# A hybrid decoder step on one core: the last token chunks 430, 430 and 172 wide, and the root of the narrow one on all partitions

## The chip, the cores and the metric

The program runs on one core of one Trainium2 chip. The metric is the device time of one execution in microseconds. The core has TensorE (PE: matmuls; PEld: its weight loads), VectorE (DVE), ScalarE (ACT), GpSimd (POOL) and SyncE (SP), which issues the DMAs; each engine works through its own queue in order, and semaphores join them.

## The reference

One layer of a decoder on 1024 prompt tokens and 8 sample tokens (1032 columns, model width 1024). The change touches the last lines alone: the second half-step FFN and the final norm.

```python
def rmsnorm(x, g):
    y = x * lax.rsqrt(jnp.mean(x * x, axis=-1, keepdims=True) + EPS)
    return y * g
...
x = x + 0.5 * swiglu(rmsnorm(x, ffn1_norm_g), ffn1_w_in, ffn1_w_out)
mix = token_mix(rmsnorm(x, mix_norm_g), ...)      # attention and DeltaNet heads
x = x + mix
gate, up = jnp.split(rmsnorm(x, ffn2_norm_g) @ ffn2_w_in, 2, axis=-1)
x = x + 0.5 * (jax.nn.silu(gate) * up) @ ffn2_w_out
y_prompt, y_sample = rmsnorm(x_prompt_rows, final_norm_g), rmsnorm(x_sample_rows, final_norm_g)
```

## The kernel before

All activations stand transposed: a tile has 128 model rows on the partitions and the 1032 tokens along its columns, so x is eight tiles of 128 x 1032, the row blocks k = 0 to 7. Float32 products are made of three reduced-precision matmuls each (`mm3`, lines 321 to 323): weights and activations are split into a high and a low part in the type float32r, and high x high, high x low and low x high are summed in PSUM. Each of the three loads its own 128x128 weights.

The program's last stage is `ffn_out` (line 706), called with `cb3`: the hidden activations, 22 blocks of 128 (`self.hs`), times the out matrix, 8 row blocks, added to x. The hidden blocks come in five groups of 4, 4, 6, 4 and 4. In the first four groups the loop runs over the row blocks m and, for each, over the three chunks of 344 tokens. In the last group it runs over the chunks first: for each chunk eight row blocks, four hidden blocks, three matmuls, 96 matmuls in all. `one` ends with VectorE's `x<-mm,x` (half the product plus x), then `square` adds up the squares: ScalarE squares into a tile `t`, and GpSimd (k = 1, 2, 3, 5, 6) or VectorE (k = 4, 7, `DVE_SQ`) adds it to `acc`.

After the eighth row block of a chunk, `cb3` starts a background job with that chunk's final norm (`norm`, line 382, `rstd`, line 360):

- three plain float32 matmuls `ps<-ones,acc` sum the squares over the partitions, token blocks of 115 as weights and one column of ones as the moving side, so that the sums come to lie on 115 partitions x 3 columns (each shows as two rows in the profile);
- VectorE makes the reciprocal root of these 115x3 numbers in twelve steps (`nv`, then `rsqrt`, line 331: a shift, a multiply-add on the bits, three rounds of three steps), and writes three diagonal matrices `t<-ident,rsqy`;
- three plain float32 matmuls `ps<-t,ones` broadcast the roots to all partitions, 344 columns (the broadcast);
- ScalarE copies the broadcast to SBUF for GpSimd; VectorE scales six row blocks, x times gain times the broadcast in PSUM (`x<-x,c_norm_g,ps`); GpSimd scales two (`POOL_Y`, k = 1 and 4) in two steps each;
- each row block is stored by a DMA `o_y<-x` on SyncE.

TensorE's queue has the order in which the program is written down. The background jobs are woven in while it is written: each matmul moves on a clock of the program's own (`tick`, line 221, a time in proportion to the columns), each step of a job books time on its engine (`book`, line 208), and the job's next piece is written down when that clock says its input is ready. The order of the other engines is set by the scheduler of the language. Tiles `t` of up to 512 columns have four buffers (`T2`), PSUM three for products and five for the rest.

Of the kernel before, what the change touches and what calls it, by code (L numbers as in the profile page):

```python
# [10 lines left out]
F32 = mybir.dt.float32  # L11
# [3 lines left out]
ALU = mybir.AluOpType  # L15
# [4 lines left out]
P = 128  # L20
D = 1024
KT = D // P
# [3 lines left out]
TT = T + NS  # L26
CW = 344
CHUNKS = [(c * CW, CW) for c in range(3)]
DFF = 2816
NF = DFF // P  # L30
NH = 4
EPS = 1e-6
BW = 1060
CONSTS = ("dist", "sink", "ssink", "conv_w", "conv_st", "negmask", "cum", "a_log", "dt_bias", "gdn_g", "sel", "kvsel")
HW = 258
# [9 lines left out]
PAD = 400.0  # L45
# [13 lines left out]
POOL_Y = (1, 4)  # L59
# [55 lines left out]
class Net:  # L115
# [83 lines left out]
        t = self.tmp.tile([P, 512], F32, tag="t2", name=self.name("t2"), bufs=T2)  # L199
        return t[:, :w]  # L200

    def pmm(self):
        return self.mm.tile([P, CW], F32, tag="mm", name=self.name("mm"))

    def pps(self):
        return self.ps.tile([P, 512], F32, tag="ps", name=self.name("ps"))
# [121 lines left out]
        lo = [self.bt(dt=F32R, s="xnlo") for _ in range(KT)]  # L328
        return hi, lo

    def rsqrt(self, x):
        nc = self.nc
        p, n = x.shape
        y = self.t("rsqy", [P, 16], bufs=3)[:p, :n]
        t = self.t("rsqt", [P, 16], bufs=2)[:p, :n]
        nc.vector.tensor_scalar(t.bitcast(I32), x.bitcast(I32), 1, None, ALU.logical_shift_right)
        nc.vector.tensor_scalar(y.bitcast(I32), t.bitcast(I32), -1.0, float(0x5F3759DF), ALU.mult, ALU.add)
        for _ in range(3):
            nc.vector.tensor_tensor(t, y, y, ALU.mult)
            nc.vector.scalar_tensor_tensor(t, t, -0.5, x, ALU.mult, ALU.mult)  # L340
            nc.vector.scalar_tensor_tensor(y, t, 1.5, y, ALU.add, ALU.mult)
        return y
# [17 lines left out]
    def rstd(self, acc, cs, use):  # L360
        nc = self.nc
        yield PAD
        m = 115 if cs[0][1] > HW else 86
        offs = [[c0, c0 + m, c0 + w - m] for c0, w in cs]
        n = 3 * len(cs)
        ps = self.pps()
        v = self.t("nv", [P, 12])
        for i, o in enumerate(sum(offs, [])):
            self.mmul(ps[:m, i:i + 1], acc[:, o:o + m], self.ones[:, 0:1])
        nc.vector.tensor_scalar(v[:m, :n], ps[:m, :n], 1.0 / D, EPS, ALU.mult, ALU.add)  # L370
        r = self.rsqrt(v[:m, :n])
        for j, (c0, w) in enumerate(cs):
            dgt = self.t2(3 * m)
            for i in range(3):
                nc.vector.tensor_scalar(dgt[:m, i * m:(i + 1) * m], self.ident[:m, :m], r[:, 3 * j + i:3 * j + i + 1], None, ALU.mult)
            yield PAD
            bcs = self.pps()
            for i, o in enumerate(offs[j]):
                self.mmul(bcs[:, o - c0:o - c0 + m], self.ones[:m, :], dgt[:m, i * m:(i + 1) * m])
            use(bcs, c0, w)  # L380

    def norm(self, x, gi, c0, w, acc, out):
        nc = self.nc

        def use(bcs, c0, w):
            rs = self.t2(w)
            nc.scalar.copy(rs[:, :w], bcs[:, :w])
            for k in range(KT):
                y = x[k][:, c0:c0 + w]
                g = self.norm_g[:, gi, k:k + 1]  # L390
                if k in POOL_Y:
                    nc.gpsimd.tensor_tensor(y, y, rs[:, :w], ALU.mult)
                    nc.gpsimd.tensor_scalar(y, y, g, 1.0, ALU.mult, ALU.mult)
                else:
                    nc.vector.scalar_tensor_tensor(y, y, g, bcs[:, :w], ALU.mult, ALU.mult)
                out(k, y)

        yield from self.rstd(acc, [(c0, w)], use)

    def scaled_split(self, x, gi, k, hi, lo, s):  # L400
        nc = self.nc
# [301 lines left out]

        self.builders.append(gen())

    def ffn_out(self, last_cb):
        nc = self.nc

        def one(m, c0, w, whi, wlo, o, f0, g):
            ps = self.pmm()  # L710
            s = slice(c0, c0 + w)
            for j in range(g):
                ks = slice(o + j * P, o + (j + 1) * P)
                h = self.need_op(self.hs, f0 + j)
                self.mm3(ps, whi[:, ks], wlo[:, ks], h[0][:, s], h[1][:, s], j == 0, j == g - 1)
            x = self.need_op(self.xr, m)
            nc.vector.scalar_tensor_tensor(x[:, s], ps, 0.5, x[:, s], ALU.mult, ALU.add)
            self.adv()

        for f0, g in KGROUPS:  # L720
            per = PER[g]
            if f0 + g < NF:
                for m0 in range(0, KT, per):
                    whi, wlo = self.take()
                    for m in range(m0, m0 + per):
                        for c0, w in CHUNKS:
                            one(m, c0, w, whi, wlo, (m - m0) * g * P, f0, g)
                    self.drop()
            else:
                wide = [(self.bt([P, per * g * P], F32R, "whi"), self.bt([P, per * g * P], F32R, "wlo")) for _ in range(KT // per - 3)]  # L730
                ws = [self.take() for _ in range(3)]
                for t in wide:
                    ws.append(self.extra(*t))
                acc = self.bt(s="acc")
                for c0, w in CHUNKS:
                    for m in range(KT):
                        whi, wlo = ws[m // per]
                        one(m, c0, w, whi, wlo, (m % per) * g * P, f0, g)
                        last_cb(self.xr, m, c0, w, None)
                        self.square(acc[:, c0:c0 + w], m, self.xr[m][:, c0:c0 + w])  # L740
                        if c0 + w == TT and m % per == per - 1:
                            if m // per < 3:
                                self.drop()
                            else:
                                self.fr(whi, wlo)
                    last_cb(self.xr, KT, c0, w, acc)
            for f in range(f0, f0 + g):
                self.fr(*self.hs[f])
# [63 lines left out]
    def chunked(self, ws, xhi, xlo, evac, jobs):  # L812
        for c, (c0, w) in enumerate(CHUNKS):
            s = slice(c0, c0 + w)
            if jobs and jobs[c][0]:
                self.wait(jobs[c][0])
            self.settle(KEEP)
            ps = [self.pps()[:, :CW] if jobs and c + i > 0 and c + i < 3 else self.pmm() for i in range(2)]
            for p, (whi, wlo) in zip(ps, ws):
                for k in range(KT):  # L820
                    ks = slice(k * P, (k + 1) * P)
                    self.mm3(p, whi[:, ks], wlo[:, ks], xhi[k][:, s], xlo[k][:, s], k == 0, k == KT - 1)
                if c == 2:
                    self.drop()
            self.due.append((jobs and jobs[c][1], partial(evac, c, *ps)))
            self.settle(KEEP if jobs else 0)

    def proj_chunk(self, wt, c, xhi, xlo, evac):
        whi, wlo = wt
        c0, w = CHUNKS[c]  # L830
        ps = self.pmm()
# [13 lines left out]
    def gates(self, xhi, xlo):  # L845
# [15 lines left out]

        for c0, w in CHUNKS:
            ps = self.pmm()
# [542 lines left out]
    def mix_in(self, xhi, xlo, rs, scr, jobs):  # L1406
# [31 lines left out]
        def evac_kv(c, pk, pv):  # L1438
            ek(pk, *CHUNKS[c])
            ev(pv, *CHUNKS[c])  # L1440
# [153 lines left out]
def build(tc, io):  # L1594
    with ExitStack() as ctx:
        ctx.enter_context(tc.manual_schedule(engines=ORDERED))
        n = Net(tc, ctx, io)
        nc = tc.nc
# [65 lines left out]
        n.mix_out(scr, xd, cb2, done2, gens, ms, ds)  # L1664
        n.ffn_head(xg, xg["rs"], done, hd[1], HEAD[1])
        n.ffn_in(xT, hd[1], lambda: n.out_ops(hd[1], lambda m: xe[:, m, :]), HEAD[1])
        n.ffn_out(cb3)
        n.wait(*jobs3)


# [88 lines left out]
```

## Time and profile before

| | |
|---|---|
| runs shown, us | 2110.12, 2114.11, 2117.31; median 2114.11 |
| the profiled execution's own time, us | 2115.43 |
| its span, first to last instruction, us | 2113.2 |
| mean granted TensorE clock over the span | 0.973 |
| PE busy, share of the span | 96% |
| DVE, ACT, POOL busy, share of the span | 58%, 33%, 28% |
| start of the last chunk's last matmul, us from the span's start | 2098.24 |

Times in the rows are microseconds from the start of the span. A matmul's row runs from its start until its last result is out, so rows of one stream overlap; what a stream costs is read from start to start. A row of the timeline with "x6" holds six like instructions in turn, from the first one's start to the last one's end.

### The profile page before, as it was taken

To read this page: it belongs to the slowest core of one execution; us is meant where nothing else is said; L and a number is where in the kernel's file an instruction comes from. 1 tells how busy PE (TensorE), PEld (TensorE's weight loads), DVE (VectorE), ACT (ScalarE), POOL (GpSimd) and SP (SyncE) were. 2 spreads that over 40 slices of the span, in tenths; PEclk is the share of its full clock that TensorE was granted. 3 is DMA by queue.
4 is the path that set the end of the run, shared out by engine and by line. 5 is a ranking of instruction groups with operands and counts; after the bars stand their busy time and mean duration, and the time that the engine had idled before them with its cause. 6 is when DMAs were issued, how large, how long until landed. Compare 5 with 4: busy or idle time off the path is not lost.

```text
span 2113.2 us, 37138 instructions
## 1 busy us (share of the span) xinstructions
PE 2024.6 (96%) x15062; PEld 1963.6 (93%) x15062; DVE 1222.1 (58%) x2624; ACT 699.8 (33%) x1491; POOL 594.9 (28%) x517
## 2 busy tenths in 40 slices
PE   7799999999999999999999979999999999999997
PEld 6799999999999998787888869899999999999997
DVE  7755555555533544676977874685555555464335
ACT  5233333333211333545243332443333333331112
POOL 3354444341000131332211111245444444200003
PEclk7999999999999999999999979999999999999999
DMA  4112222227322221211212151221222222552112
GB/s 152 60 58 91 81 73 84 86 71 281 113 68 60 84 81 35 69 45 32 67 46 50 57 181 35 97 70 61 86 81 83 79 81 76 194 195 84 55 41 81
DMA packets 109771, 180.81 MB, mean 86 GB/s; under 512 B 35168, under 2 KB 63744, under 8 KB 109584
## 3 DMA queue, kind: packets, MB, share of 16 engines
q1 hardware_dynamic: 109568, 178.41, 26.6%
q8 instruction: 118, 1.93, 0.4%
q14 instruction: 53, 0.43, 0.1%
q0 software_dynamic: 32, 0.03, 0.0%
HBM read 135.60 MB, written 43.85 MB: 85 GB/s over the span
## 4 chain that ended last, share of the span: by engine, by line
PE 40%; DVE 8%; DMA 1%; issue 1%; SPq 1%; ACT 0%; POOL 0%; DVEq 0%; ACTq 0%; POOLq 0%
PE mm L321 6%; PE mm L322 6%; PE mm L323 6%; PE ps L528 4%; PE ps L530 4%; PE ps L529 4%; PE ps L243 3%; PE mm L528 2%; PE mm L530 2%; PE mm L529 2%; DVE conv L89 1%; DVE inv L89 1%; SPq L102 1%; DVE Tb L89 1%; DVE x L89 1%
## 5 line engine op out<-in xcount | busy, mean ns | idle before, releaser
L528 PE MATMUL ps<-xhi,wop 128*128 128x258 f32 x1480 | 421.0, 284 | 7.4 <-DVE sw L89 7.2
L530 PE MATMUL ps<-xhi,wop 128*128 128x258 f32 x1480 | 419.3, 283 | 0.0
L529 PE MATMUL ps<-xlo,wop 128*128 128x258 f32 x1480 | 419.3, 283 | 0.0
L321 PE MATMUL mm<-hhi,hi 128*128 128x344 f32 x1008 | 322.3, 320 | 0.0
L322 PE MATMUL mm<-hlo,hi 128*128 128x344 f32 x1008 | 322.3, 320 | 0.0
L323 PE MATMUL mm<-hhi,lo 128*128 128x344 f32 x1008 | 321.6, 319 | 0.0
L89 DVE TENSOR_TENSOR wop<-r,wop 128x512 fp32r<-128x512 f32 x185 | 158.5, 859 | 253.9 <-ACT wop L89 239.8
L528 PEld LDWEIGHTS ps<-xhi,wop 128*128 128x128 f32 x1480 | 280.9, 190 | 8.7 <-issue 7.2
L529 PEld LDWEIGHTS ps<-xlo,wop 128*128 128x128 f32 x1480 | 281.9, 191 | 0.0
L530 PEld LDWEIGHTS ps<-xhi,wop 128*128 128x128 f32 x1480 | 281.2, 190 | 0.0
L89 DVE SCALAR_TENSOR_TENSOR x<-mm,x 128x344 f32<-128x344 f32 x240 | 123.3, 515 | 220.0 <-PE mm L323 217.9
L89 ACT CAST hi<-raw 128x1024 fp32r<-128x1024 f32 (+1 forms) x78 | 76.7, 984 | 357.0 <-PE mm L322 327.0
L321 PEld LDWEIGHTS mm<-hhi,hi 128*128 128x128 f32 x1008 | 189.4, 188 | 0.3 <-DVE x L89 0.3
L323 PEld LDWEIGHTS mm<-hhi,lo 128*128 128x128 f32 x1008 | 189.4, 188 | 0.0
L322 PEld LDWEIGHTS mm<-hlo,hi 128*128 128x128 f32 x1008 | 189.3, 188 | 0.0
L89 POOL TENSOR_TENSOR acc<-acc,t 128x344 f32<-128x344 f32 (+1 forms) x50 | 45.5, 911 | 508.2 <-ACT t L89 495.9
L321 PE MATMUL mm<-xnhi,hi 128*128 128x344 f32 x488 | 172.1, 353 | 0.0
L528 PE MATMUL mm<-xhi,wop 128*128 128x258 f32 x592 | 167.5, 283 | 0.0
L530 PE MATMUL mm<-xhi,wop 128*128 128x258 f32 x592 | 167.2, 283 | 0.0
L529 PE MATMUL mm<-xlo,wop 128*128 128x258 f32 x592 | 167.0, 282 | 0.0
L89 ACT CAST wop<-r 128x512 fp32r<-128x512 f32 x185 | 114.7, 621 | 144.6 <-PE mm L530 77.0
L323 PE MATMUL mm<-xnhi,lo 128*128 128x344 f32 x488 | 158.6, 325 | 0.0
(320 smaller groups left out, 4607.5 us busy)
## 6 DMA issues: line engine op xcount, KB each, us to landing
r<-in_w_in SPq DMA_DIRECT2D x86, 512.0 KB, 3.6
hraw<-hd SPq DMA_DIRECT2D x44, 516.0 KB, 5.0
hd<-sw SPq DMA_DIRECT2D x74, 258.0 KB, 2.0
raw<-in_w_out SPq DMA_DIRECT2D x34, 512.0 KB, 4.0
raw<-in_w_mix SPq DMA_DIRECT2D x22, 512.0 KB, 3.6
raw<-in_w_out SPq DMA_DIRECT2D x24, 384.0 KB, 3.2
x<-in_x SPq DMA_DIRECT2D x16, 516.0 KB, 9.0
xd<-x SPq DMA_DIRECT2D x24, 172.0 KB, 1.9
```

The lines of the kernel that those rows point to most:

```text
L89: return fn(out, *a, **k)
L102: return self.eng.dma_start(out, src)
L243: self.nc.tensor.matmul(out, lhsT, rhs, start=start, stop=stop)
L321: mm(ps, whi, xhi, start=start, stop=False)
L322: mm(ps, whi, xlo, start=False, stop=False)
L323: mm(ps, wlo, xhi, start=False, stop=stop)
L528: mm(ps, w[:, a], x[0][:, c], start=first, stop=False, skip_group_check=True)
L529: mm(ps, w[:, a], x[1][:, c], start=False, stop=False, skip_group_check=True)
L530: mm(ps, wlo, x[0][:, c], start=False, stop=last, skip_group_check=True)
```

## The change

The last group of `ffn_out`'s second call goes over chunks of 430, 430 and 172 tokens instead of three of 344; the four groups ahead of it keep 344. The PSUM tiles of the products are cut out of 512 columns. `rstd` takes as many token blocks as the chunk needs: four of 108 for 430 tokens, three of 115 or 86 as before elsewhere. A chunk of up to 256 tokens has a norm of its own: one plain float32 matmul with the 128x128 ones as weights puts the sums of the squares on all partitions, and the root is taken there, on 128 x 172 numbers, in three `t` tiles; no diagonals, no broadcast, no copy. The scaling then reads the root from SBUF.

```diff
@@ -26,6 +26,7 @@
 TT = T + NS
 CW = 344
 CHUNKS = [(c * CW, CW) for c in range(3)]
+LAST = [(0, 430), (430, 430), (860, 172)]
 DFF = 2816
 NF = DFF // P
 NH = 4
@@ -199,8 +200,8 @@
         t = self.tmp.tile([P, 512], F32, tag="t2", name=self.name("t2"), bufs=T2)
         return t[:, :w]
 
-    def pmm(self):
-        return self.mm.tile([P, CW], F32, tag="mm", name=self.name("mm"))
+    def pmm(self, w=CW):
+        return self.mm.tile([P, 512], F32, tag="mm", name=self.name("mm"))[:, :w]
 
     def pps(self):
         return self.ps.tile([P, 512], F32, tag="ps", name=self.name("ps"))
@@ -328,11 +329,12 @@
         lo = [self.bt(dt=F32R, s="xnlo") for _ in range(KT)]
         return hi, lo
 
-    def rsqrt(self, x):
+    def rsqrt(self, x, y=None, t=None):
         nc = self.nc
         p, n = x.shape
-        y = self.t("rsqy", [P, 16], bufs=3)[:p, :n]
-        t = self.t("rsqt", [P, 16], bufs=2)[:p, :n]
+        if y is None:
+            y = self.t("rsqy", [P, 16], bufs=3)[:p, :n]
+            t = self.t("rsqt", [P, 16], bufs=2)[:p, :n]
         nc.vector.tensor_scalar(t.bitcast(I32), x.bitcast(I32), 1, None, ALU.logical_shift_right)
         nc.vector.tensor_scalar(y.bitcast(I32), t.bitcast(I32), -1.0, float(0x5F3759DF), ALU.mult, ALU.add)
         for _ in range(3):
@@ -360,9 +362,10 @@
     def rstd(self, acc, cs, use):
         nc = self.nc
         yield PAD
-        m = 115 if cs[0][1] > HW else 86
-        offs = [[c0, c0 + m, c0 + w - m] for c0, w in cs]
-        n = 3 * len(cs)
+        q = -(-cs[0][1] // P)
+        m = -(-cs[0][1] // q)
+        offs = [[c0 + min(i * m, w - m) for i in range(q)] for c0, w in cs]
+        n = q * len(cs)
         ps = self.pps()
         v = self.t("nv", [P, 12])
         for i, o in enumerate(sum(offs, [])):
@@ -370,9 +373,9 @@
         nc.vector.tensor_scalar(v[:m, :n], ps[:m, :n], 1.0 / D, EPS, ALU.mult, ALU.add)
         r = self.rsqrt(v[:m, :n])
         for j, (c0, w) in enumerate(cs):
-            dgt = self.t2(3 * m)
-            for i in range(3):
-                nc.vector.tensor_scalar(dgt[:m, i * m:(i + 1) * m], self.ident[:m, :m], r[:, 3 * j + i:3 * j + i + 1], None, ALU.mult)
+            dgt = self.t2(q * m)
+            for i in range(q):
+                nc.vector.tensor_scalar(dgt[:m, i * m:(i + 1) * m], self.ident[:m, :m], r[:, q * j + i:q * j + i + 1], None, ALU.mult)
             yield PAD
             bcs = self.pps()
             for i, o in enumerate(offs[j]):
@@ -395,7 +398,24 @@
                     nc.vector.scalar_tensor_tensor(y, y, g, bcs[:, :w], ALU.mult, ALU.mult)
                 out(k, y)
 
-        yield from self.rstd(acc, [(c0, w)], use)
+        if w > 2 * P:
+            yield from self.rstd(acc, [(c0, w)], use)
+            return
+        yield PAD
+        ps = self.pps()[:, :w]
+        self.mmul(ps, self.ones, acc[:, c0:c0 + w])
+        v = self.t2(w)
+        nc.vector.tensor_scalar(v, ps, 1.0 / D, EPS, ALU.mult, ALU.add)
+        r = self.rsqrt(v, self.t2(w), self.t2(w))
+        for k in range(KT):
+            y = x[k][:, c0:c0 + w]
+            g = self.norm_g[:, gi, k:k + 1]
+            if k in POOL_Y:
+                nc.gpsimd.tensor_tensor(y, y, r, ALU.mult)
+                nc.gpsimd.tensor_scalar(y, y, g, 1.0, ALU.mult, ALU.mult)
+            else:
+                nc.vector.scalar_tensor_tensor(y, y, g, r, ALU.mult, ALU.mult)
+            out(k, y)
 
     def scaled_split(self, x, gi, k, hi, lo, s):
         nc = self.nc
@@ -703,11 +723,11 @@
 
         self.builders.append(gen())
 
-    def ffn_out(self, last_cb):
+    def ffn_out(self, last_cb, chunks=CHUNKS):
         nc = self.nc
 
         def one(m, c0, w, whi, wlo, o, f0, g):
-            ps = self.pmm()
+            ps = self.pmm(w)
             s = slice(c0, c0 + w)
             for j in range(g):
                 ks = slice(o + j * P, o + (j + 1) * P)
@@ -732,7 +752,7 @@
                 for t in wide:
                     ws.append(self.extra(*t))
                 acc = self.bt(s="acc")
-                for c0, w in CHUNKS:
+                for c0, w in chunks:
                     for m in range(KT):
                         whi, wlo = ws[m // per]
                         one(m, c0, w, whi, wlo, (m % per) * g * P, f0, g)
@@ -1664,7 +1684,7 @@
         n.mix_out(scr, xd, cb2, done2, gens, ms, ds)
         n.ffn_head(xg, xg["rs"], done, hd[1], HEAD[1])
         n.ffn_in(xT, hd[1], lambda: n.out_ops(hd[1], lambda m: xe[:, m, :]), HEAD[1])
-        n.ffn_out(cb3)
+        n.ffn_out(cb3, LAST)
         n.wait(*jobs3)
 
 
```

What moves: up to the last group the five engines' queues are the same before and after. In the last group two places differ in order, not only in widths.

TensorE, the second chunk's broadcast (`ps<-t,ones`), before; `mm_22148` and `mm_22189` are products of the third chunk, 51 matmuls of which still follow:

```order
L321 MATMUL mm_22148<-hhi_21398,hi_21660 128x344
L322 MATMUL mm_22148<-hlo_21399,hi_21660 128x344
L323 MATMUL mm_22148<-hhi_21398,lo_21661 128x344
L243 MATMUL ps_22158<-t_2914_22114,ones 128x115 x3
L321 MATMUL mm_22148<-hhi_21418,hi_21660 128x344
L322 MATMUL mm_22148<-hlo_21419,hi_21660 128x344
L323 MATMUL mm_22148<-hhi_21418,lo_21661 128x344
```

TensorE, the end of the stream, after; `mm_22221` is the last product of the narrow chunk, `ps_22234` the second chunk's broadcast, `ps_22263` the narrow chunk's sums:

```order
L323 MATMUL mm_22221<-hlo_21399,whi_21754 128x172
L324 MATMUL mm_22221<-hhi_21398,wlo_21755 128x172
L322 MATMUL mm_22221<-hhi_21418,whi_21754 128x172
L323 MATMUL mm_22221<-hlo_21419,whi_21754 128x172
L324 MATMUL mm_22221<-hhi_21418,wlo_21755 128x172
L244 MATMUL ps_22234<-t_2916_22144,ones 128x108 x4
L244 MATMUL ps_22263<-acc_21760,ones 128x172
```

The broadcast has moved from the middle of the third chunk behind its last matmul.

VectorE, from the last product of the third chunk on, before; `acc` is the addition of the last squares, `nv` the first step of the root:

```order
L89 SCALAR_TENSOR_TENSOR x_20036<-mm_22240,x_20036 128x344
L89 TENSOR_TENSOR acc_21760<-acc_21760,t_2929_22254 128x344
L89 TENSOR_SCALAR nv_22258<-ps_22257 115x3
L89 TENSOR_SCALAR rsqt_22264<-nv_22258 115x3
L89 TENSOR_SCALAR rsqy_22263<-rsqt_22264 115x3
L89 TENSOR_TENSOR rsqt_22264<-rsqy_22263 115x3
```

VectorE from the same place on, after; `c_norm_g,ps_22234` are the scalings of the second chunk, `t_2931_22265<-ps_22263` is the first step of the narrow chunk's root:

```order
L90 SCALAR_TENSOR_TENSOR x_20036<-mm_22221,x_20036 128x172
L90 SCALAR_TENSOR_TENSOR x_19936<-x_19936,c_norm_g,ps_22234 128x430
L90 SCALAR_TENSOR_TENSOR x_19966<-x_19966,c_norm_g,ps_22234 128x430
L90 SCALAR_TENSOR_TENSOR x_19968<-x_19968,c_norm_g,ps_22234 128x430
L90 SCALAR_TENSOR_TENSOR x_20000<-x_20000,c_norm_g,ps_22234 128x430
L90 SCALAR_TENSOR_TENSOR x_20034<-x_20034,c_norm_g,ps_22234 128x430
L90 SCALAR_TENSOR_TENSOR x_20036<-x_20036,c_norm_g,ps_22234 128x430
L90 TENSOR_TENSOR acc_21760<-acc_21760,t_2929_22260 128x172
L90 TENSOR_SCALAR t_2931_22265<-ps_22263 128x172
L90 TENSOR_SCALAR t_2933_22268<-t_2931_22265 128x172
```

The six scalings of the second chunk, which stood ahead of the last four products of the third chunk, now stand between the last product and the addition of the last squares. The stores of the narrow chunk come in the order k = 0, 2, 3, 1, 4, 5, 6, 7 (1 and 4 are GpSimd's); before it was 0, 2, 3, 5, 1, 4, 6, 7.

## Rows read from the trace of the kernel before

**Rows 1.** Stretches: us, busy us (instructions) by engine, granted clock, DMA share, GB/s.

```profile
2048.00:2098.40 50.40, 50.40 (x329) 50.27 (x327) 28.57 (x74) 13.25 (x26) 19.04 (x23) 1.00 0.16 57
2098.40:2113.20 14.80, 2.52 (x13) 2.03 (x12) 6.63 (x23) 0.94 (x2) 3.33 (x5) 0.67 0.27 95
```

**Rows 2.** TensorE's timeline, tail: start, us, instruction, count, [idle before, releaser].

```profile
2098.24 0.32 PE L323 MATMUL mm<-hhi,wlo 128*128 128x344 f32 x1
2100.36 0.76 PE L243 MATMUL ps<-ones,acc 128*115 128x1 f32 x6 [1.81 <-DVE acc L89]
2103.96 1.60 PE L243 MATMUL ps<-t,ones 115*128 115x115 f32 x6 [2.83 <-DVE t L89]
```

**Rows 3.** Timeline of VectorE in the tail.

```profile
2099.79 0.52 DVE L89 TENSOR_TENSOR acc<-acc,t 128x344 f32<-128x344 f32 x1 [0.69 <-ACT t L89]
2101.16 0.16 DVE L89 TENSOR_SCALAR nv<-ps 115x3 f32<-115x3 f32 x1 [0.86 <-PE ps L243]
...
2103.33 0.16 DVE L89 SCALAR_TENSOR_TENSOR rsqy<-rsqt,rsqy 115x3 f32<-115x3 f32 x1
...
2106.13 2.99 DVE L89 SCALAR_TENSOR_TENSOR x<-x,c_norm_g,ps 128x344 f32<-128x344 f32 x6 [1.94 <-ACT t L89]
```

**Rows 4.** Timeline of ScalarE, GpSimd and SyncE in the tail.

```profile
2105.65 0.45 ACT L89 COPY t<-ps 128x344 f32<-128x344 f32 x1 [5.96 <-PE ps L243]
...
2106.17 1.78 POOL L89 TENSOR_TENSOR x<-x,t 128x344 f32<-128x344 f32 x2 [7.28 <-ACT t L89]
2106.73 3.79 SPq L1651 DMA_DIRECT2D o_y<-x  x8
2107.93 1.08 POOL L89 TENSOR_SCALAR x<-x,c_norm_g 128x344 f32<-128x344 f32 x2
```

**Rows 5.** Timeline of TensorE, first and 19th of a run, 258 and 344 columns.

```profile
343.82 0.28 PE L529 MATMUL ps<-xlo,wop 128*128 128x258 f32 x1
...
345.97 0.28 PE L529 MATMUL mm<-xlo,wop 128*128 128x258 f32 x1
...
2085.44 0.32 PE L321 MATMUL mm<-hhi,hi 128*128 128x344 f32 x1
...
2088.28 0.32 PE L321 MATMUL mm<-hhi,hi 128*128 128x344 f32 x1
```

**Rows 6.** Timeline of TensorE's weight loads.

```profile
1017.99 1.90 PEld L243 LDWEIGHTS ps<-qn,st 128*128 128x128 f32 x16
1019.82 0.19 PEld L321 LDWEIGHTS mm<-xnhi,hi 128*128 128x128 f32 x1
...
2084.85 0.19 PEld L321 LDWEIGHTS mm<-hhi,hi 128*128 128x128 f32 x1
2084.96 0.19 PEld L322 LDWEIGHTS mm<-hlo,hi 128*128 128x128 f32 x1
```

**Rows 7.** Timeline around a broadcast in the stream, TensorE and ScalarE.

```profile
2089.53 0.32 PE L323 MATMUL mm<-hhi,lo 128*128 128x344 f32 x1
2089.69 0.82 PE L243 MATMUL ps<-t,ones 115*128 115x115 f32 x6
2090.27 0.40 PE L321 MATMUL mm<-hhi,hi 128*128 128x344 f32 x1
...
2090.60 0.45 ACT L89 COPY t<-ps 128x344 f32<-128x344 f32 x1 [0.18 <-PE ps L243]
```

**Rows 8.** Groups of VectorE instructions by shape: count, busy us, mean ns, idle before.

```profile
L89 DVE SCALAR_TENSOR_TENSOR x<-x,c_norm_g,ps 128x258 f32<-128x258 f32 x64 | 26.1, 473 | 1.9 <-ACT rs L89 1.9
...
L89 DVE SCALAR_TENSOR_TENSOR x<-x,c_norm_g,ps 128x344 f32<-128x344 f32 x18 | 9.0, 567 | 1.9 <-ACT t L89 1.9
```

**Rows 9.** A group of GpSimd instructions by shape.

```profile
L89 POOL TENSOR_TENSOR sw<-sw 128x258 f32<-128x258 f32 x74 | 54.5, 739 | 30.4 <-ACT sw L89 30.2
```

**Rows 10.** Timeline of GpSimd and VectorE in the third chunk.

```profile
2087.77 0.92 POOL L89 TENSOR_TENSOR acc<-acc,t 128x344 f32<-128x344 f32 x1 [5.29 <-ACT t L89]
...
2087.80 0.92 DVE L89 SCALAR_TENSOR_TENSOR rsqy<-rsqt,rsqy 115x3 f32<-115x3 f32 x1
```

## The prediction

> **What bounds the kernel now.** Read the table by stretches [rows 1] first. Up to 2098.4 us TensorE is busy in all of the last 50 us at a granted clock of 1.00, its upper level of 2.4 GHz; the 14.8 us behind that hold 2.52 us of TensorE and a mean clock of 0.67. So two things can move the end: the time that the matmul stream of the last group of hidden blocks takes, and the length of the tail behind it. Everything ahead of that group is the same program, instruction by instruction, on all five engines.
>
> In the tail, go by engine. The last matmul of the stream starts at 2098.24; the sums run at 2100.36, the broadcast at 2103.96 [rows 2]. Between them VectorE does the last addition, then twelve small steps of the root, 2101.16 to 2103.33, 0.197 us from start to start; then the diagonals and, after ScalarE's copy, the six scalings in 2.99 us [rows 3]. GpSimd scales its two row blocks beside them, and SyncE issues eight stores in 3.79 us, 0.474 each [rows 4]. From the end of the last issue, 2110.52, to the end of the span at 2113.2 are 2.68 us. Counted from the start of the last stream matmul the tail is 2113.2 - 2098.24 = 14.96 us. I call that moment zero below.
>
> **The change, 1: the stream.** 288 matmuls of 344 columns become 192 of 430 and 96 of 172; the columns are the same. What one costs is read from starts, not durations, because matmuls overlap: 18 steps from 2085.44 to 2088.28 are 0.158 us each at 344 columns; 18 from 343.82 to 345.97 are 0.119 at 258 [rows 5]. The line through both has 0.45 ns a column and nearly no fixed part, so 430 columns cost 0.196, and 172 would cost 0.081: 192 and 96 of them take what the 288 took. But each matmul also loads 128x128 weights. Where matmuls of one column leave nothing else to do, 16 such loads keep 0.114 us from each other; and where the stream restarts behind an interlude, the second load of the reduced-precision kind follows the first after 0.11 [rows 6]. At 344 and 258 columns the load hides under the streaming of the matmul before; at 172 it doesn't. I bound the narrow step by 0.081 below (load hidden) and 0.31 above (rival B), and take 0.114, since that row has the same size of load. Price: 96 x (0.114 - 0.081) = **+3.2 us**.
>
> The interludes: a broadcast between matmuls takes 2090.27 - 2089.53 - 0.16 = 0.58 us with six rows, two for each of three blocks [rows 7]. The wide chunks have four blocks, so eight rows, about 0.2 more, and so have the sums. Before, two sums and two broadcasts stood in the stream; now two sums and one broadcast do: 3 x 0.2 - 0.58, **nothing**. The first broadcast comes 24 matmuls, 4.7 us, behind its sums, where 30 x 0.158 = 4.7 us stood before: VectorE's root fits as before.
>
> **The change, 2: the tail.** The order shows the point. The second chunk's broadcast stood 51 matmuls ahead of the end of the stream; now it comes after the last matmul of the stream, and VectorE has the six 430-wide scalings of that chunk ahead of the last addition of the narrow chunk's squares. So a whole chunk's scaling, which had the third chunk's matmuls as cover, lies bare. From zero:
>
> - Copy of the broadcast starts: in the stream this took 2090.60 - 2089.53 = 1.07 us [rows 7]; two rows more and a shorter matmul ahead give 1.24.
> - VectorE starts 0.48 behind the copy's start (2105.65 to 2106.13 [rows 3, 4]); 86 more columns on ScalarE, +0.1: 1.82.
> - Six scalings: 0.567 us at 344 columns and 0.473 at 258 is 1.09 ns a column [rows 8]; the step of 0.484 becomes 0.578, six take 3.47: 5.29.
> - The last addition: 0.52 us at 344 columns, 0.34 at 172, and a hop to TensorE of 0.05: 5.68.
> - One plain float32 matmul with the ones as weights, two rows of 172 columns. Bounds: six rows of 115 took 0.82 us at the upper clock level [rows 7] and 1.60 in the tail, at the lower [rows 2]; a step of 0.10 or 0.22 scaled to 172 columns, twice, with the last row's run-out gives 0.45 or 0.9. TensorE will have idled over 4 us, as before its slow broadcast; I take 0.7: 6.42.
> - The root on 128 x 172: twelve dependent steps. A step of 3 columns takes 0.197; the addition's 0.52 at 344 against 0.16 at 3 is 1.04 ns a column, so 172 columns add 0.176: 12 x 0.373 = 4.48. Before: 2.37, and the diagonals and second broadcast behind it, which go. 10.90.
> - Scale and store. GpSimd's product costs 0.89 at 344 columns [rows 4] and 0.74 at 258 [rows 9], so 0.57 at 172; its second step, by the half of 0.54 and a fixed part, 0.43. The fourth store in SyncE's order waits for GpSimd's first row block: free of VectorE that is ready 1.6 us behind the root. It won't be free. Before, the scaling read the broadcast from PSUM; now both its inputs lie in SBUF. A three-column step of the root that met a GpSimd addition took 0.92 us instead of 0.16 [rows 3] and ended with it [rows 10]. So the six scalings and GpSimd's four take turns, each of its first three steps behind a scaling, for some 0.2 of it bare, and the block is ready at about 2.1. Then five issues of 0.474 and 2.68 us to the end: 2.2 + 2.4 + 2.7, 7.2 in all: 18.1.
>
> The tail grows from 14.96 to 18.1, **+3.1 us**, between +2.2 (upper clock, no turns) and +4. The Trainium skill says why turns are taken: in "SBUF — State Buffer", section Who interferes with whom, a VectorE instruction with two SBUF inputs contends with a GpSimd one that reads SBUF, and the one that comes second waits it out. The rows 10 agree; without that rule the tail would come to 17.6.
>
> Sum: 3.2 + 0 + 3.1 = +6.3 on the profiled execution's 2115.43, so 2121.7. The median of the runs shown, 2114.11, is 1.3 lower: **2120.4 us**, +0.3%. A measurement of this kernel tells a change from none at about 0.3%, 6.3 us: my sum lies on that line.
>
> **Rivals.** A, the load is hidden after all: the narrow step is 0.081, the stream costs nothing, the sum is the tail's +3.1: 2117.2. For it: loads do overlap matmuls everywhere in the stream. Against: the 0.114 between bare loads. The Trainium skill, "TensorE: Matmul & The Clock Gate", section Back-to-back issue gap, gives N/2.4 + 2.5 ns, 74 ns at 172 columns; as an estimate from that page, the end would come at 2116.5; no run here shows it at that width.
>
> B, on the slow side: below some width the reduced-precision matmul loses its rate and goes like a plain float32 one. Plain rows of 115 columns are 0.104 apart and a matmul is two of them [rows 7]: 1.8 ns a column, 0.31 us at 172. Price 96 x (0.31 - 0.114) = +18.8: 2139. It decides if the limit lies between 172 and 258, the narrowest in this program. Against it: 258 and 344 lie on one line with no fixed part, so nothing is seen to set in.
>
> C, also slower: with a third of its time spent on loads, TensorE falls to the lower clock level in the narrow chunk. 172 columns at 1.2 GHz are 0.143 and more: 96 x 0.035 = +3.4, 2123.8.
>
> D, faster: the tail shrinks with the chunk, as if the second chunk were done. Then nothing of 430 columns stands there: from zero to the sums 2.1 us before [rows 2], three steps half as wide, so 1.6; matmul 0.7, root 4.5, stores 7.2, together 14.0. That is 1.0 less than before, and with the +3.2 of the stream still 2116.3. To be faster by 6 us, the stream would have to speed up too, and no row offers that.
>
> **How the numbers follow.** My sum 0.71, A 0.12, B 0.09, C 0.05, D or some other gain 0.03. The sum's own uncertainty of 1 to 2 us falls on both sides of the line, half and half. Slower by over 0.3%: 0.36 + B + C = 0.50; within: 0.35 + A = 0.47; faster: 0.03. The range reaches from A with the tail's lower bound, 2115.5, to C with its upper one, 2125; B is left out.
>
> **What would show it.** Narrow matmuls 0.114 apart (0.08 or 0.31 would be A or B; a clock under 1.00 ahead of the last one, C); the second chunk's six scalings behind the last stream matmul, 0.58 apart; the root's steps 0.37 apart; scalings of 172 columns that last longer than 0.34 where GpSimd works; the last store issued 15.4 us behind zero. Wrong it is if the narrow chunk's squares are added before those six scalings, or if the span's growth lies ahead of 2050 us.

## The result, and the profile after

The changed kernel takes 2120.51 us (median of 22 runs, 2115.02 to 2128.79); the kernel before, beside it, 2116.51 (median of 22, 2107.06 to 2126.95). The ratio is 1.0028, with a 95% interval of 1.0015 to 1.0041: slower by 0.28%, some 5.9 us (3.2 to 8.7; the two medians lie 4.0 apart, the two means 5.9), which lies on the line that the prediction drew.

Single executions scatter by more than that, so the comparison below goes by the length of stages, each read from one profiled execution. The first profiled execution of the changed kernel has a span of 2122.2 us (before: 2113.2) at a mean granted clock of 0.968. The first matmul of the last group starts at 2053.88, before at 2050.46: 3.4 of the 9.0 us of difference lie where both programs are the same, and a second profile of either kernel moves that start by 2 to 3 us again. Behind it the stages of two profiles of the same kernel differ by 0.4 us at most (see the experiments). TensorE's timeline of the changed kernel, the start of the last group, then a stretch of the narrow chunk:

```profile
2053.72 0.32 PE L324 MATMUL mm<-hhi,lo 128*128 128x344 f32 x1
2053.88 0.35 PE L322 MATMUL mm<-hhi,hi 128*128 128x430 f32 x1
...
2093.28 0.28 PE L324 MATMUL mm<-hhi,lo 128*128 128x172 f32 x1
2093.39 0.28 PE L322 MATMUL mm<-hhi,hi 128*128 128x172 f32 x1
2093.50 0.28 PE L323 MATMUL mm<-hlo,hi 128*128 128x172 f32 x1
...
2096.96 0.28 PE L324 MATMUL mm<-hhi,lo 128*128 128x172 f32 x1
```

From 2093.28 to 2096.96 are 33 steps of 0.1115 us. The stretches that answer to [rows 1], up to the last stream matmul and behind it:

```profile
2053.80:2104.60 50.80, 50.80 (x315) 49.33 (x314) 26.08 (x68) 12.82 (x25) 16.15 (x19) 1.00 0.10 36
2104.60:2122.20 17.60, 1.94 (x11) 1.33 (x10) 10.80 (x26) 0.76 (x2) 5.60 (x9) 0.58 0.40 140
```

The granted clock is 1.00, the upper level, through the narrow chunk as well. In the tail VectorE is busy for 10.80 us of 17.60; before it was 6.63 of 14.80. From the timeline of all engines in the tail (answers to [rows 2 to 4]):

```profile
2104.42 0.28 PE L324 MATMUL mm<-hhi,wlo 128*128 128x172 f32 x1
...
2104.53 1.07 PE L244 MATMUL ps<-t,ones 108*128 108x108 f32 x8
2104.73 0.34 DVE L90 SCALAR_TENSOR_TENSOR x<-mm,x 128x172 f32<-128x172 f32 x1 [1.00 <-PE mm L324]
2105.69 0.52 ACT L90 COPY t<-ps 128x430 f32<-128x430 f32 x1 [1.52 <-PE ps L244]
...
2106.25 3.52 DVE L90 SCALAR_TENSOR_TENSOR x<-x,c_norm_g,ps 128x430 f32<-128x430 f32 x6 [1.18 <-ACT t L90]
...
2106.93 12.80 SPq L1671 DMA_DIRECT2D o_y<-x  x16
...
2109.69 0.33 DVE L90 TENSOR_TENSOR acc<-acc,t 128x172 f32<-128x172 f32 x1
...
2110.07 0.94 PE L244 MATMUL ps<-acc,ones 128*128 128x172 f32 x2 [4.47 <-DVE acc L90]
2111.05 0.34 DVE L90 TENSOR_SCALAR t<-ps 128x172 f32<-128x172 f32 x1 [1.04 <-PE ps L244]
...
2114.67 0.71 DVE L90 SCALAR_TENSOR_TENSOR t<-t,t 128x172 f32<-128x172 f32 x2
2115.41 2.82 DVE L90 SCALAR_TENSOR_TENSOR x<-x,c_norm_g,t 128x172 f32<-128x172 f32 x6
2115.46 1.35 POOL L90 TENSOR_TENSOR x<-x,t 128x172 f32<-128x172 f32 x2 [6.11 <-DVE t L90]
```

The second chunk's six scalings (2106.25) stand between the last product (2104.73) and the last addition (2109.69), and TensorE waits 4.47 us for that addition. The stream, from the first matmul of the last group to the start of its last, goes from 2098.24 - 2050.46 = 47.78 us to 2104.42 - 2053.88 = 50.54; the tail, from there to the end of the span, from 15.01 (14.96 in the prediction, by the rounded span) to 17.81. Together **+5.6 us**, half by half.

### The profile page after: what moved, and what is told of

Read it like the earlier page. It is cut to its first block, busy times and chain, and to the rows that moved or that the text cites. A ratio compares the mean times of both kernels' runs of the same rounds, so it can differ in the third digit from the quotient of the medians.

```text
span 2122.2 us, 37133 instructions
## 1 busy us (share of the span) xinstructions
PE 2031.9 (96%) x15060; PEld 1969.2 (93%) x15060; DVE 1224.2 (58%) x2623; ACT 699.1 (33%) x1490; POOL 591.9 (28%) x517
## 4 chain that ended last, share of the span: by engine, by line
PE 39%; DVE 8%; issue 1%; DMA 1%; SPq 1%; ACT 0%; POOL 0%; DVEq 0%; ACTq 0%; POOLq 0%
PE mm L322 6%; PE mm L323 6%; PE mm L324 6%; PE ps L548 4%; PE ps L550 4%; PE ps L549 4%; PE ps L244 3%; PE mm L548 2%; PE mm L550 2%; PE mm L549 2%; DVE conv L90 1%; DVE inv L90 1%; DVE x L90 1%; DVE Tb L90 1%; DVE xglo L90 1%
## 5 line engine op out<-in xcount | busy, mean ns | idle before, releaser
L323 PE MATMUL mm<-hlo,hi 128*128 128x344 f32 (+2 forms) x1008 | 323.1, 321 | 0.0
L322 PE MATMUL mm<-hhi,hi 128*128 128x344 f32 (+2 forms) x1008 | 322.9, 320 | 0.0
L324 PE MATMUL mm<-hhi,lo 128*128 128x344 f32 (+2 forms) x1008 | 322.5, 320 | 0.0
L90 DVE SCALAR_TENSOR_TENSOR x<-mm,x 128x344 f32<-128x344 f32 (+2 forms) x240 | 123.2, 515 | 224.4 <-PE mm L324 222.6
L90 POOL TENSOR_TENSOR acc<-acc,t 128x258 f32<-128x258 f32 (+3 forms) x50 | 44.7, 895 | 513.6 <-ACT t L90 503.1
```

The costliest lines, as they stand in the source:

```text
L90: return fn(out, *a, **k)
L322: mm(ps, whi, xhi, start=start, stop=False)
L323: mm(ps, whi, xlo, start=False, stop=False)
L324: mm(ps, wlo, xhi, start=False, stop=stop)
```

## The experiments

The stages of each kernel's profiled execution, us:

| kernel | stream | tail | sum |
|---|---|---|---|
| before | 47.78 | 15.01 | 62.79 |
| before, once more | 47.78 | 15.41 | 63.18 |
| changed | 50.54 | 17.81 | 68.35 |
| changed, once more | 50.54 | 17.80 | 68.35 |
| changed, old root | 50.54 | 17.21 | 67.75 |
| 344 wide, wide root | 47.78 | 18.72 | 66.49 |
| changed, broadcast 33 matmuls ahead of the end | 51.43 | 15.44 | 66.87 |
| changed, broadcast 45 ahead | 53.01 | 13.56 | 66.57 |
| changed, no GpSimd in the last scalings | 50.54 | 17.57 | 68.11 |
| 500, 500, 32 | 61.16 | 19.76 | 80.92 |
| 388, 386, 258, wide root | 48.59 | 17.12 | 65.71 |
| 388, 386, 258, old root | 48.59 | 15.59 | 64.18 |
| before, two store queues | 47.78 | 15.23 | 63.01 |

**How far stages scatter.** Both kernels were profiled once more, unchanged.

> The kernel before, unchanged: a second profile, to see how far the lengths of single stages scatter from one execution to the next. Zero is the start of the last stream matmul. Mine: the stream of the last group (from the first of its 288 matmuls to the start of the last) again takes 47.8 us and the tail 15.0, each within 0.2 us, while the whole span may lie some us off the first profile's 2113.2. Rival: the stages scatter as the whole run does, by several us; then the +2.8 and +2.8 us read from one pair of profiles would mean little.

> The changed kernel once more, for the scatter of its stages. Mine: stream 50.5 us within 0.1, tail 17.8 within 0.4 (the part of it in which TensorE's clock has fallen or not yet differs from one execution to the next). Rival: the tail scatters by more than 1 us, and the +2.8 is not a property of the kernel.

The streams came out the same to 0.01 us. The changed kernel's tail did too; that of the kernel before came out 0.4 longer. TensorE's timeline of its second profile shows where (compare [rows 2], where the sums took 0.76):

```profile
2095.60 0.32 PE L323 MATMUL mm<-hhi,wlo 128*128 128x344 f32 x1
...
2097.72 1.15 PE L243 MATMUL ps<-ones,acc 128*115 128x1 f32 x6 [1.81 <-DVE acc L89]
```

The granted clock over those sums is 0.60; in the first profile it was 1.00 there. TensorE has run dry by then, and its clock falls a little earlier or later. So a tail is read to 0.4 us, and the change is worth 5.2 to 5.6 us by stages: both parts of it are real.

**Is it the wide root?** The narrow chunk with the old root:

```diff
-        if w > 2 * P:
+        if w > 0:
             yield from self.rstd(acc, [(c0, w)], use)
```

> Chunks 430, 430 and 172 as in the changed kernel, but the narrow chunk takes the old root (two token blocks of 86, sums, twelve small steps, diagonals, broadcast, copy). Mine: the stream stays at 50.5 us, since the weight loads and the widths are unchanged; the second chunk's broadcast stays behind the stream, and the tail comes to 17.2 us (16.8 to 17.6), 0.6 under the changed kernel's 17.8, because the small root's steps cost 0.2 and not 0.36, and the two blocks' diagonals, broadcast and copy eat most of that. Rival, the wide root is what lengthens the tail: then the tail falls under 16 us, back towards the 15.0 of before.

The tail was 17.21, as expected, and the rival (under 16) is out: of the 2.8 us that the tail grew, the wide root makes 0.6. From the first step of the root to the first scaling the wide root takes 4.36 us (2111.05 to 2115.41), the old one here 4.21 (2110.03 to the scalings at 2114.24, shown further on):

```profile
2110.03 0.15 DVE L90 TENSOR_SCALAR nv<-ps 86x2 f32<-86x2 f32 x1 [0.83 <-PE ps L244]
```

The other half of the question, the kernel before with the wide root in its last chunk alone (`LAST` not passed):

```diff
-        if w > 2 * P:
+        if c0 + w < TT:
             yield from self.rstd(acc, [(c0, w)], use)
```

> Three chunks of 344 as before, but the last one takes its root on all partitions, 128 x 344. Mine: the stream stays at 47.8 us, the second chunk's broadcast stays covered, and the tail comes to 18.2 us, 3.2 over before: twelve steps of about 0.55 (6.6 us) in place of the small root, the diagonals, the broadcast and the copy, and scalings in turns with GpSimd behind them. So the wide root by itself saves nothing at this width. Rival, the wide root is the gain of the change and the uncovered broadcast its only loss: the tail falls under 14.5 us.

It came to 18.72, 0.5 over the figure, 3.3 to 3.7 over the kernel before, and the rival (under 14.5) is out. VectorE's timeline:

```profile
2098.05 0.52 DVE L90 TENSOR_SCALAR t<-ps 128x344 f32<-128x344 f32 x1 [1.30 <-PE ps L244]
...
2104.31 5.00 DVE L90 SCALAR_TENSOR_TENSOR x<-x,c_norm_g,t 128x344 f32<-128x344 f32 x6
```

From the first step of the root to the first scaling it takes 6.26 us there; the old root with its diagonals, broadcast and copy took 4.97 (2101.16 to 2106.13 in [rows 3]). Then the scalings last 5.00 us instead of 2.99. So what a root on all partitions saves in small steps it pays per column, and at both widths it is the slower one.

**Is it the uncovered scaling?** Nothing is changed here but the place at which the second chunk's norm is written down:

```diff
-        self.tick(int(xhi.shape[1]) * 3 / 2.36)
+        n = int(xhi.shape[1])
+        self.tick((262 if n == 172 else n) * 3 / 2.36)
```

> The changed kernel, with the program's own clock charging a matmul of 172 columns as one of 262, so that the second chunk's broadcast is written down 33 matmuls ahead of the end of the stream. No work is added or left out. Mine: the uncovered scaling of the second chunk is most of the tail's growth, so the tail falls from 17.8 to 14.0 us (13.6 to 14.5); the broadcast now lies in the stream, which goes to 51.2 (+0.6). Together 65.2 us against 68.35 in the changed kernel and 62.8 before: +2.4 us on before, 0.1%, no difference that a measurement tells. Rival, the wide root makes the tail: it stays at 17 us or more.

The tail fell by 2.4 us and not by 3.8: the direction was right and the rival (17 or more) is out, but the size was wrong. VectorE's timeline:

```profile
2098.26 3.53 DVE L90 SCALAR_TENSOR_TENSOR x<-x,c_norm_g,ps 128x430 f32<-128x430 f32 x6 [0.39 <-ACT t L90]
...
2101.70 0.82 DVE L90 SCALAR_TENSOR_TENSOR x<-mm,x 128x172 f32<-128x172 f32 x3
...
2103.70 0.34 DVE L90 TENSOR_TENSOR acc<-acc,t 128x172 f32<-128x172 f32 x1 [1.18 <-POOL acc L90]
```

The last stream matmul starts at 2101.01. The scalings end 0.8 us behind it, and three products have piled up behind them (the row "x3"), with their squares and GpSimd's additions still to come, so the last addition comes at +2.7 (in the next kernel, at +1.2). Over ten runs the whole time is 2119.04 us, ratio 1.0016 (0.9996 to 1.0037), in keeping with +4.1 us by stages. Hence the next kernel, with 330 in the place of 262:

> The changed kernel with the program's clock charging a narrow matmul as 330 columns: the second chunk's sums are written down after 18 and its broadcast after 51 narrow matmuls, 45 ahead of the end of the stream instead of 33. Mine: the chain of the second chunk's norm, from its last matmul to its last scaling, is by now longer (about 12 us) than the whole narrow chunk (96 x 0.111 and an interlude, 11.5 us), so writing it down earlier only makes TensorE wait for VectorE. The stream grows to 52.5 us (52.1 to 52.8) and the tail shrinks to 14.3 (14.0 to 14.8); the sum stays at 66.8 (66.4 to 67.2), as with the broadcast 33 ahead. Rival, the place of the broadcast is all that matters: the stream stays at 51.4, the tail falls to 14.0, the sum to 65.4.

The sum, 66.57, is what was expected; stream and tail went a little further apart than their ranges, 53.01 and 13.56. All of the scaling is covered now: the sums start at 2103.42, 1.60 us behind the last stream matmul (in the kernel before 2.12). That tail is 1.4 to 1.8 shorter than that of the kernel before. But TensorE pays for it. Its waits between 2088 and 2102 (the same list of the changed kernel, from 2088 to 2105, is empty):

```profile
PE mm L322 <- DVE x L90: 0.8, 1, 0.8
PE ps L244 <- DVE acc L90: 0.3, 1, 0.3
```

and the chain that it waits for, in the timeline:

```profile
2087.82 0.36 PE L324 MATMUL mm<-hhi,wlo 128*128 128x430 f32 x1
...
2090.43 0.92 PE L244 MATMUL ps<-ones,acc 128*108 128x1 f32 x8 [0.28 <-DVE acc L90]
...
2094.95 1.09 PE L244 MATMUL ps<-t,ones 108*128 108x108 f32 x8
2096.13 0.52 ACT L90 COPY t<-ps 128x430 f32<-128x430 f32 x1
2096.68 3.53 DVE L90 SCALAR_TENSOR_TENSOR x<-x,c_norm_g,ps 128x430 f32<-128x430 f32 x6 [1.00 <-ACT t L90]
...
2103.42 0.56 PE L244 MATMUL ps<-acc,ones 128*128 128x172 f32 x2 [1.33 <-DVE acc L90]
```

From the last 430-wide matmul, 2087.82, to the end of its last scaling, 2100.21, the norm of a 430-wide chunk takes 12.4 us. The narrow chunk is 96 x 0.1115 = 10.7 us of matmuls; with the sums and the broadcast that interrupt it, it lasts about as long as the norm, 12.4 us in the kernel with the broadcast 33 ahead (2088.59 to 2101.01). So nothing is left over. Written late, the norm sticks out behind the stream; written early, it makes TensorE wait for the sums and, while VectorE scales and takes no product out of PSUM, for a free product buffer. Over the changed kernel the stream has grown by 2.47: read from start to start, the longer stop at the sums is 0.5 of it, the wait for the buffer 1.0 and the broadcast itself 0.9. At both places the sum comes to 66.6 to 66.9, and the rival, that only the place matters, is out. Places between the two, and scalings that take turns with the products on VectorE, were not tried.

**Is it the weight load?** The narrowest chunk was made 32 wide, `LAST = [(0, 500), (500, 500), (1000, 32)]`.

> Chunks of 500, 500 and 32 tokens, the last with the wide root. Mine: a narrow matmul with its own 128x128 weights costs what the load costs, whatever its columns, so the 96 matmuls of 32 columns are 0.111 us apart, as those of 172 were; 500 columns cost 0.227; the stream takes about 56 us. Rival, the step follows columns with another factor below some width: 0.111 x 32/172 = 0.02 us a step and a stream of some 47 us. Second rival, a lower rate for narrow matmuls with a fixed rate per column (0.111/172 = 0.65 ns a column): the same 0.02 us.

TensorE's timeline at the head of that chunk and further on:

```profile
2105.94 0.26 PE L324 MATMUL mm<-hhi,lo 128*128 128x32 f32 x1
...
2110.41 0.26 PE L322 MATMUL mm<-hhi,hi 128*128 128x32 f32 x1
...
2110.84 0.38 PE L322 MATMUL mm<-hhi,hi 128*128 128x32 f32 x1
2111.06 0.38 PE L323 MATMUL mm<-hlo,hi 128*128 128x32 f32 x1
...
2121.51 0.37 PE L324 MATMUL mm<-hhi,wlo 128*128 128x32 f32 x1
```

The first 40 steps take 4.47 us, 0.112 each: a fifth of the columns and the same step, so the rivals by which it follows the columns are out. A fixed cost of 0.11 us for any matmul would look the same in this run; against it stands that sums with fewer columns of weights follow each other faster (the last section). The stream was not 56 us, though, but 61.16, for a reason that none of the three had. The stretches, the first up to 2110.6 and the second behind it:

```profile
2105.80:2110.60 4.80, 4.80 (x45) 4.79 (x43) 1.93 (x5) 1.31 (x4) 0.51 (x3) 1.00 0.00 0
2110.60:2121.60 11.00, 11.00 (x54) 11.00 (x53) 0.96 (x5) 0.92 (x4) 0.99 (x4) 0.50 0.01 1
```

At 2110.6, with TensorE busy and waiting for nothing, the granted clock falls to 0.50, the lower level of 1.2 GHz, and from 2110.84 to 2121.51 the step is 50 times 0.213, which makes 5.1 of the missing 5.2 us. This is rival C of the prediction, at a width where it does happen; at 172 columns it does not.

A last chunk wide enough to hide the load, `LAST = [(0, 388), (388, 386), (774, 258)]` and the wide root for 258:

> Chunks of 388, 386 and 258 tokens, the last with the wide root on 128 x 258. Mine: at 258 columns the load hides under the matmul before it, so the narrow step is 0.119 us, by columns alone, and the stream takes 48.6 us; the second chunk's broadcast lies 33 matmuls ahead of the end, so its scaling is covered and the tail is what the wide root makes it, 12 x 0.46 and scalings in turns: 16.4 us. Sum 65.0, +2.2 on before. Rival, any uneven split costs the stream about 3 us: 50.5 or more.

The stream was 48.59, to the digit: an uneven split by itself costs 0.8 us, and the rival (50.5 or more) is out; a load that isn't hidden does. The tail was 17.12, 0.7 more than I had: the scalings end at 2103.93, level with the last stream matmul (2103.83), and again three products wait behind them. With the old root at the same split (`if w > 0`, as above):

> Chunks of 388, 386 and 258 tokens with the old root everywhere (for the last, three token blocks of 86). Mine: the stream is 48.6 us as with the wide root at this split; the tail falls from 17.1 to 15.3 us (14.9 to 15.8), since the small root saves 0.7 us up to the first scaling and the scalings from PSUM take no turns with GpSimd. Sum 63.9, 1.1 over the kernel before. Rival, a last chunk narrower than 344 shortens the tail in proportion once the weight loads are hidden: the sum falls under 62.8.

The tail came to 15.59, within its range, and the sum to 64.18, 1.0 to 1.4 over the kernel before. The rival is out: at this split the tail isn't shorter than before (15.0 to 15.4), let alone in proportion. Here too the second chunk's scalings end only with the stream; this split with an earlier broadcast was not tried.

**Do VectorE and GpSimd take turns?** The last scalings all on VectorE:

```diff
-            if k in POOL_Y:
+            if k in ():
                 nc.gpsimd.tensor_tensor(y, y, r, ALU.mult)
```

> The changed kernel, with all eight scalings of the narrow chunk on VectorE and none on GpSimd. Mine: the 0.47 us from scaling to scaling there are turns that VectorE takes with GpSimd; alone it does a scaling of 172 columns in 0.31 us or less (0.28 to 0.34), eight in 2.5. The end moves by at most 0.3 us, since SyncE's eight issues of 0.474 bound it then. Rival, a scaling whose three inputs lie in SBUF takes 0.47 by itself: the step stays at 0.47, eight take 3.8, and the tail grows by 0.5 to 1 us.

VectorE's row of the scalings in this kernel, and (below) in the one with the old root, whose scalings read the broadcast from PSUM beside GpSimd's:

```profile
2108.04 2.56 DVE L90 SCALAR_TENSOR_TENSOR x<-x,c_norm_g,t 128x172 f32<-128x172 f32 x8
```

```profile
2114.24 1.91 DVE L90 SCALAR_TENSOR_TENSOR x<-x,c_norm_g,ps 128x172 f32<-128x172 f32 x6 [1.47 <-ACT t L90]
```

That is 0.32 us a scaling in both, against 2.82 / 6 = 0.47 where both happen at once: inputs in SBUF and GpSimd at work. So it takes both, and the rival is out. The section of the Trainium skill's "SBUF — State Buffer" that the prediction names has it so too. The tail shrinks by 0.24, within the 0.3 expected.

**A version that beats both?** In the kernel before, the tail seemed to end with eight issues in a row [rows 4]. So its last stores were split between two queues:

```diff
...
+                    q = nc.scalar if c0 + w == TT and k in (2, 4, 5, 7) else nc.sync
+                    q.dma_start(io["o_y"][:, k, c0:c0 + w], y)
...
```

> The kernel before, with the eight stores of its last chunk split between two queues: four issued by ScalarE, four by SyncE. Mine: the tail of the kernel before ends with eight issues of 0.474 us in a row on SyncE; with two queues the last issue follows its scaling at once, and the tail goes from 15.0 to 14.1 us. In the whole time that is 0.04%, no difference that a measurement tells. Rival, the stores are bound by the transfers behind them: the tail stays at 15.0.

The rival has it: 15.23, and 2113.18 us over 12 runs, ratio 0.9994 (0.9976 to 1.0012). The first scaling starts at 2103.64 and the span ends at 2110.76: 7.12 us, as in the kernel before (2106.13 to 2113.25). The view of the DMA engines says why, 40 slices from 2103 to 2111 in this kernel, then from 2105 to 2113.3 in the kernel before; a digit is the busy share in tenths:

```profile
DMA  0000000000598799999999999999980000000000
```

```profile
DMA  0000000000005999999999999999999400000000
```

The 1.41 MB keep the DMA engines full for some 4 us either way. And no split of the tokens tried here comes under the 62.8 to 63.2 us of the kernel before.

## Why the prediction was right, step by step

- **The stream, +3.2 us forecast, +2.76 measured.** The mechanism held: the weight load sets the narrow step. It is 0.1115 us, not the 0.114 taken: 96 x (0.1115 - 0.081) = 2.9. The interludes and the wide steps, put at nothing, give 0.2 back. Rivals A (0.081) and B (0.31) are out. The Trainium skill, "TensorE: Matmul & The Clock Gate", gives 74 ns by the formula in its section Back-to-back issue gap, which by that section's own words leaves the load out; its section LDWEIGHTS (loading the stationary operand) says that a load goes by the columns of the weights, and as an estimate from its figure 128 of them take 107 ns. The measured 0.1115 sides with the load.
- **The lower clock in the narrow chunk (C).** Not at 172 columns, where the granted clock stays at 1.00; it did come at 32. The rows read for the prediction could not tell these two apart.
- **The uncovered scaling, from zero.** The copy starts at +1.27 (forecast 1.24), the scalings at +1.83 (1.82), the last addition at +5.27 (5.29), the sums at +5.65 (5.68): all as worked out. That the cover was lost to the order, and that the cover alone is worth more than what the root costs, is shown by the kernel with the broadcast 45 ahead (tail 13.56, near rival D's 14.0, at a price of 2.47 in the stream) and by the old root (17.21). What the prediction didn't see is that neither of the two earlier places gives the cover for nothing, since the norm of 430 columns takes as long as the whole narrow chunk.
- **Sums and root.** The sums' matmul was mis-sized: the first step of the root starts at +6.63 instead of +6.42. It ran at the lower clock (row of 0.94 us; where the clock was still up, in the kernel with the broadcast 45 ahead, 0.56). The twelve steps take 4.36, 0.363 each, instead of 4.48.
- **Scalings and stores, 7.2 forecast, 6.82 measured** (2115.41 to 2122.23). Turns are taken, 0.47 us a scaling, but without GpSimd the end comes 0.24 earlier and not the 0.5 that I gave the turns; and from the last issue to the end are 2.5 us, not 2.68. I took the issues for the bound of this stretch in both kernels. In the kernel before it was the transfers (the run with two queues). In the narrow chunk, with half the bytes, the DMA engines are not full and the issues go out 0.474 apart, so there the issues look like the bound, though no run with that chunk took them away. With half the bytes the stretch is hardly shorter than the 7.1 us of the kernel before. The same view of the changed kernel, 40 slices from 2113.25 to 2122.25:

```profile
DMA  0000000000000006509239392929393840000000
```

- **Sum: 18.1 for the tail against 17.81, +6.3 in all against +5.6** (5.2 by the second profile of before) by stages and 5.9 (3.2 to 8.7) in the whole time. Cut at the first step of the root and the first scaling, the tail's +2.80 is +3.71 ahead of the root, -0.61 in it and -0.30 behind it. The median, 2120.51, lies at the forecast 2120.4; but the forecast started from a median of 2114.11, the kernel before came to 2116.51 this time, and single medians scatter by some us. So that closeness is luck, while the sum is not.
- **The range.** By the prediction's own terms its lower end, rival A with the tail's lower bound, is 2114.1 + 2.2 = 2116.3 and not 2115.5. Nothing above hangs on it.

## What to carry to other kernels

A float32r matmul with its own 128 columns of weights cost the larger of its own streaming (0.45 ns a column) and the load (0.1115 us) here, while the clock was at its upper level. By these two figures the load takes over below some 250 columns (258 was measured on the one side, 172 and 32 on the other), and a narrower chunk saves TensorE nothing. And a smaller last chunk shortens the tail only if it is still longer than what runs in its shadow: here the norm of the chunk ahead of it took 12.4 us, and 10.7 us of matmuls did not cover it without loss at either of the two earlier places tried. Before counting on a shorter last step, add up the chain that the last-but-one step leaves behind.

## What the runs showed that was not expected

- TensorE's granted clock fell to the lower level in the middle of an unbroken stream, 4.8 us into the 32-wide matmuls. The step went from 0.112 to 0.213 us with it. A busy TensorE is not by itself a TensorE at the upper level.
- A load goes by the columns of the weights. Where the clock was up, the six rows of the sums with 115 columns of weights and one column to stream took 0.76 us [rows 2], 0.101 from start to start; with 86 columns, at the 258 split with the old root, 0.62 and 0.077:

```profile
2100.67 0.62 PE L244 MATMUL ps<-ones,acc 128*86 128x1 f32 x6 [2.97 <-DVE acc L90]
```

- A wait for a product buffer can come from scalings: six of them on VectorE, 3.5 us, held up the products long enough for TensorE to stop for 0.8 us.
